# Strassen block products with three token groups in place of plain products for the merge and the MLP of a hybrid recurrent block

## The chip, the cores and the metric

One Trainium2 chip, one of its cores. The metric is the device time of one execution in microseconds. TensorE (PE, with its weight loads PEld), VectorE (DVE), ScalarE (ACT), GpSimd (POOL) and the DMA queues of SyncE (SP) and ScalarE work side by side and wait for each other on semaphores.

## What is computed

One layer over 2048 latent tokens and 256 context tokens of width 1024, then a final norm. The part that matters here is what follows the recurrences:

```python
def branch_merge(h_lru, g, p_mixed, gt, w_lru_out, w_pool_out, w_o):
    lru_out = (h_lru * jax.nn.gelu(g)) @ w_lru_out          # z @ [1024,1024]
    pool_out = p_mixed @ w_pool_out                         # y @ [512,1024]
    g_lru, g_pool = jnp.split(jax.nn.sigmoid(gt), N_BRANCH, axis=-1)
    return (g_lru * lru_out + g_pool * pool_out) @ w_o      # [1024,1024]
...
x = x + gate1[:, None, :] * y_l
x = x + gate2[:, None, :] * sq_relu_mlp(modulate(x, norm2_g[l], shift2, scale2), mlp_w1[l], mlp_w2[l])
...
def sq_relu_mlp(h, w1, w2):                                 # w1 [1024,4096], w2 [4096,1024]
    return jnp.square(jax.nn.relu(h @ w1)) @ w2
```

## The kernel before

Channels stand on the 128 partitions, tokens on the free dimension. Every product of two float32 matrices is run as three float16 passes (high by high, high by low, low by high, `mm3`, L65 to L73) over operands scaled by a power of two (`scale_of`, L75: a POOL all-reduce at L81 and three tiny DVE instructions) and split into halves (`split`, L93: ACT writes the high half at L94, DVE the low half at L95). One matmul takes a 128x128 weight block and 512 tokens.

The first part (to about 1086 us) computes the normed input, the recurrences, the gates and the pool branch. It leaves z (8 tiles of 128 channels), y (4 tiles) and the sigmoid gates s in DRAM. It ends with gate tiles ("fills", L422) whose matmuls read the normed input.

Then comes the second part. y and z are reloaded and split (`reload`, L715); `w_pool_out` with y (L740), `w_lru_out` with z (L758) and the gates give the merged tiles `mt`; `w_o` (L808) adds to x and gives `x1`; `make_h2` norms it. The MLP runs over 16 groups of 256 hidden channels and 4 blocks of 512 tokens: `m1` (L833 takes the result out of PSUM), `m1_split` (DVE and ACT make the two halves of the hidden values), `m2` (L868 adds each product to `x1`). Weights are loaded, scaled and split once (`prep`, L102), a group ahead. POOL has little to do here but all-reduces.

The order on each engine is set by the scheduler of the tile layer from the program's order and its own model of time; SP's DMA queue alone keeps the program's order. Tiles come from pools with a fixed number of buffers, and a new tile waits until an old one's last reader is done.

Of the kernel before, what the change touches and what calls it, by code (L numbers as in the profile page):

```python
# [17 lines left out]
P = 128  # L18
# [21 lines left out]

@with_exitstack
def block_kernel(ctx: ExitStack, tc: tile.TileContext, a):
    """Activations keep channels on partitions and tokens on the free dimension.

    Matrix products run as three float16 passes (hi*hi + hi*lo + lo*hi) over operands that are
    scaled by powers of two taken from their measured magnitude and split into two halves.
    """
# [9 lines left out]
    apool = ctx.enter_context(pool("apool", 1))  # L57
    ring = ctx.enter_context(pool("ring", 4))
# [7 lines left out]
    # ---------------------------------------------------------------- helpers  # L66
# [8 lines left out]
    def scale_of(m, k):  # L75
        with tc.high_priority(offset=PRIO):
            return scale_of_(m, k)

    def scale_of_(m, k):
# [5 lines left out]
        V.tensor_scalar(inv.bitcast(I32), e, 14 << 23, 20 << 23, op0=OP.subtract, op1=OP.max)  # L85
# [16 lines left out]
    def prep(srcs, joint=False, w16=None):  # L102
        """Load chunks [128, n <= 1024]; each gets its own scale, or all of them one."""
# [27 lines left out]
    icnt = cp.tile([P, 5, 64], F32, name="icnt")  # L131
    nc.sync.dma_start(icnt, a["icnt"])
# [19 lines left out]
    # 8*softplus(-lam): max(-lam, 0) + log1p(exp(-|lam|)), log1p(e) = 2 atanh(e / (2 + e))  # L152
# [24 lines left out]
    # ---------------------------------------------------------------- scratch in DRAM  # L177
# [5 lines left out]
    mmax = cp.tile([P, NB, KT], F32, name="mmax")  # L183
# [3 lines left out]
    st = ExitStack()  # L187
    slots = st.enter_context(pool("slots", 10, reuse_waits="tile"))
# [13 lines left out]
    def rstd(total, w, rs):  # L202
        """1 / sqrt(mean + eps) on every partition of sums of squares [128, w] per partition."""
# [6 lines left out]
    def rstd_of(x, w, t_tile):  # L210
        """The same of x [128, 8, w]."""
# [37 lines left out]
    def norm_x(x, w, eng):  # L249
        """Its inverse root mean square and a supply of pieces, both in one slot."""  # L250
# [26 lines left out]
    # shift1 and scale1 for the latent and the context stream  # L277
# [17 lines left out]
    def ada1_pe(wt, cc):  # L295
        """As rows on two partitions, then turned into columns."""
# [11 lines left out]
    def ada1_dve(wt, c):  # L308
        """Products summed over k on VectorE, then over partitions."""
# [30 lines left out]
    def affine(scale, shift, g, m):  # L340
        """Scaled per-channel factor and term of a modulated norm, and the inverse scale."""
# [6 lines left out]
        s, inv = scale_of(bd[:, 0:1], 1)  # L348
# [35 lines left out]
    def ada_piece(q):  # L384
        """gate1, shift2, scale2, gate2 (q = 0..3) of the latent stream."""
# [21 lines left out]
    class Fill:  # L407
        """Sigmoid of one tile of branch-gate channels, kept in DRAM for the merge."""
# [24 lines left out]
    class Lru:  # L433
        """One tile of 128 recurrent channels: conv, gates, both scans, gelu gate."""
# [44 lines left out]
        def gates(self, between=()):  # L479
            """Recurrence and input gates; the products of other tiles go in between."""  # L480
# [59 lines left out]
    # first tiles, token block by token block as the normed input becomes ready  # L540
# [79 lines left out]
    # ---------------------------------------------------------------- pool branch  # L620
# [67 lines left out]
    fetch(("y", 0), a["w_po"][0])  # L688
# [26 lines left out]
    def reload(src, s, hi, lo):  # L715
        for q in range(0, T, 1024):
            raw = ring.tile([P, 1024], F32, name="raw")
            nc.sync.dma_start(raw, src[:, q:q + 1024])
            split(hi[:, q:q + 1024], lo[:, q:q + 1024], raw, s)

    def tokens(b):
        return slice(b * BW, b * BW + BW)

    y16 = ywp.tile([P, 2, 4, T], F16, name="yw")
# [18 lines left out]
    wo16 = ywp.tile([P, KT, 2, 1024], F16, name="yw")
    inv_wo = cp.tile([P, KT], F32, name="inv_wo")
    for n in range(KT):
        if n + 1 < KT:
            fetch(("z", n + 1), a["w_lo"][n + 1])
        (w,), invw = wq.pop(("z", n))
        iv = mul_small(invw, inv_z, 1, "ivf")
        _, iw = prep([a["w_o"][n]], w16=[wo16[:, n]])  # L750
        V.tensor_copy(inv_wo[:, n:n + 1], iw)
        for b in range(NB):
            t = t512()
            nc.sync.dma_start(t, s_d[0][n][:, tokens(b)])
            ps = ptile()
            mm3(ps, wt8(w), [(z16[k // 2][:, 0, k % 2, tokens(b)], z16[k // 2][:, 1, k % 2, tokens(b)])
                             for k in range(KT)])
            V.scalar_tensor_tensor(t, ps, iv, t, op0=OP.mult, op1=OP.mult)  # L758
            V.tensor_tensor(mt[b][:, n, :], mt[b][:, n, :], t, op=OP.add)
            absmax(mmax[:, b, n:n + 1], mt[b][:, n, :])  # L760

    # ================================================================ w_o, residual, second norm
    aff2 = affine(mod2[:, 2, :], mod2[:, 1, :], vc("g2"), 2)
    inv_h2 = aff2[2]
    x1 = []
    h2 = []

    def make_h2(b):
        rs = rstd_of(x1[b], BW, t512)
        t = bpool.tile([P, KT, 2, BW], F16, name=f"B{b}")  # L770
        modulate(x1[b], BW, rs, aff2[0], aff2[1], t, t512)
        h2.append(t)

    NG = 16

    def prep_w1(g):
        w1, inv1 = prep([a["w1"][2 * g], a["w1"][2 * g + 1]], joint=True)
        return w1, mul_small(inv1, inv_h2, 1, "iv1")

    m16s, css = [], []  # L780

    def split_m(b):
        mx = sm.tile([P, 1], F32, name="um")
        absmax(mx, mmax[:, b, :])
        s, inv = scale_of(mx, 1)
        cs = sm.tile([P, KT], F32, name="cs")
        V.scalar_tensor_tensor(cs, inv_wo, inv, mod2[:, 0, :], op0=OP.mult, op1=OP.mult)
        m16 = bpool.tile([P, KT, 2, BW], F16, name=f"B{b}")
        for k in range(KT):
            split(m16[:, k, 0, :], m16[:, k, 1, :], mt[b][:, k, :], s)  # L790
        xt = apool.tile([P, KT, BW], F32, name=f"A{b}")
        nc.sync.dma_start(xt, a["xT"][b])
        x1.append(xt)
        m16s.append(m16)
        css.append(cs)
# [205 lines left out]
```

## Time and profile before

| what | us |
|---|---|
| three runs | 2883.71, 2883.86, 2886.08 |
| median | 2883.86 |
| profiled execution: its span (no other time of it is given) | 2885.5 |
| of it, first part, to the last fill | 1086 |
| of it, second part | 1799 |
| PE busy in the span | 2721.1 |

[...] PE matmuls are pipelined: what one costs in a stream is the distance from one to the next, not its own length.

### The profile page before, as it was taken

How to read it: one execution, taken by the hardware profiler on the slowest of the kernel's cores; microseconds unless marked ns; L12 is line 12 of the kernel's file. 1: busy time of each engine (PE TensorE's matmuls, PEld its weight loads, DVE VectorE, ACT ScalarE, POOL GpSimd, SP SyncE). 2: the span in 40 equal slices, each digit the busy share in tenths (PEclk: the TensorE clock that was granted, in tenths of full speed). 3: DMA queues.
4: the chain of work that ended last, by engine and by line, in shares of the span. 5: the costliest groups of instructions: out<-in, count | busy, mean ns of one | idle time of the engine just before them, and what ended most of it. 6: DMA issues, size and time to landing. Idle time of an engine off the chain costs nothing.

```text
span 2885.5 us, 30620 instructions
## 1 busy us (share of the span) xinstructions
PE 2721.1 (94%) x12496; PEld 1241.8 (43%) x12496; DVE 1904.9 (66%) x2883; ACT 812.7 (28%) x917; POOL 459.1 (16%) x371
## 2 busy tenths in 40 slices
PE   5798988898889999999997999999999999999998
PEld 1344444444334444444443444444444444444444
DVE  4867778875576745676466666666666665656567
ACT  2655564446545232113231111011011110110112
POOL 2713332332322000000331000000000000000022
PEclk7899999999999999999999999999999999999999
DMA  7021123211111136433001000000000000000002
GB/s 304 9 77 59 70 99 113 88 51 55 55 41 40 55 121 222 154 105 132 30 18 56 30 30 29 16 30 25 20 30 30 30 16 29 30 22 23 0 30 88
DMA packets 49165, 177.60 MB, mean 62 GB/s; under 512 B 4736, under 2 KB 7040, under 8 KB 43520
## 3 DMA queue, kind: packets, MB, share of 16 engines
q1 hardware_dynamic: 44992, 146.29, 14.9%
q10 hardware_dynamic: 4032, 29.36, 2.5%
q8 instruction: 97, 1.59, 0.2%
q14 instruction: 44, 0.36, 0.0%
HBM read 137.88 MB, written 37.75 MB: 61 GB/s over the span
## 4 chain that ended last, share of the span: by engine, by line
PE 66%; DVE 13%; issue 7%; ACT 6%; POOL 5%; DMA 3%; SPq 0%; ACTq 0%; DVEq 0%; POOLq 0%
PE mm L72 65%; DVE slot L515 2%; POOL slot L513 2%; POOL sc_g L81 1%; DMA raw<-z 1%; DVE slot L518 1%; DVE slot L512 1%; DVE slot L395 1%; DVE wm L91 1%; POOL slot L535 1%; ACT slot L493 1%; DVE A L868 1%; DVE slot L471 1%; ACT slot L94 1%; POOL slot L257 1%
## 5 line engine op out<-in xcount | busy, mean ns | idle before, releaser
L72 PEld LDWEIGHTS <-w 128*128 128x128 f16 x10944 | 1078.1, 99 | 1387.2 <-issue 136.9
L72 PE MATMUL mm<-B,w 128*128 128x512 f16 x3840 | 845.6, 381 | 15.1 <-ACT B L233 5.3
L72 PE MATMUL mm<-A,w 128*128 128x512 f16 x3408 | 774.3, 388 | 72.2 <-ACT slot L422 56.8
L72 PE MATMUL mm<-h,w 128*128 128x512 f16 (+1 forms) x3120 | 676.4, 376 | 9.7 <-DVE h L858 9.5
L868 DVE SCALAR_TENSOR_TENSOR A<-mm,cs,A 128x512 f32<-128x512 f32 (+1 forms) x520 | 373.6, 738 | 44.2 <-PE mm L72 42.5
L833 DVE TENSOR_SCALAR_CACHE_REDUCE r<-mm 128x512 f32<-128x512 f32 x128 | 88.2, 689 | 309.8 <-PE mm L72 309.7
L855 ACT ACTIVATE h<-r 128x1024 f16<-128x1024 f32 x64 | 67.6, 1056 | 791.4 <-DVE ivs L850 766.0
L94 ACT ACTIVATE w<-raw,sc_s 128x1024 f16<-128x1024 f32 (+1 forms) x116 | 127.1, 1116 | 458.9 <-PE mm L72 260.2
L91 DVE TENSOR_REDUCE wm<-raw 128x1 f32<-128x1024 f32 (+1 forms) x124 | 146.2, 1181 | 123.9 <-DMA raw<-in_w_dram 78.5
L72 PE MATMUL mm<-B,yw 128*128 128x512 f16 x768 | 166.4, 379 | 0.0
L841 POOL PARTITION_ALL_REDUCE hm<-um x64 | 23.1, 361 | 865.9 <-DVE um L839 841.9
L95 DVE SCALAR_TENSOR_TENSOR w<-raw,sc_s,w 128x1024 f16<-128x1024 f32 (+1 forms) x116 | 143.1, 1253 | 26.7 <-ACT w L94 26.2
L72 PE MATMUL mm<-slot,g 128*128 128x512 f16 (+1 forms) x528 | 118.6, 373 | 4.9 <-ACT slot L493 4.9
L81 POOL PARTITION_ALL_REDUCE sc_g<-wm x69 | 65.6, 973 | 308.6 <-DVE wm L91 249.8
L72 PEld LDWEIGHTS <-yw 128*128 128x128 f16 x768 | 75.1, 98 | 91.6 <-issue 1.7
L493 ACT ACTIVATE slot<-mm,vec,ivg 128x512 f32<-128x512 f32 (+1 forms) x160 | 105.0, 743 | 10.9 <-PE mm L72 9.8
L498 POOL TENSOR_TENSOR slot<-slot 128x2312 f32<-128x2312 f32 x16 | 83.6, 5223 | 117.5 <-ACT slot L493 115.3
L94 ACT ACTIVATE slot<-slot,sc_s 128x2312 f16<-128x2312 f32 (+1 forms) x12 | 25.8, 2148 | 258.9 <-DVE sc_s L87 240.2
L512 DVE SCALAR_TENSOR_TENSOR slot<-slot 128x2312 f32<-128x2312 f32 x16 | 41.0, 2562 | 82.7 <-ACT slot L511 82.7
L72 PE MATMUL mm<-yw,w 128*128 128x512 f16 x384 | 83.4, 379 | 0.3 <-DVE w L95 0.2
L72 PEld LDWEIGHTS <-g 128*128 128x128 f16 x528 | 53.9, 102 | 65.5 <-issue 13.1
L858 DVE TENSOR_TENSOR h<-sq,h 128x1024 f16<-128x1024 f32 x64 | 77.9, 1217 | 0.0
(182 smaller groups left out, 2108.1 us busy)
## 6 DMA issues: line engine op xcount, KB each, us to landing
raw<-in_w_dram SPq DMA_DIRECT2D x64, 512.0 KB, 3.2
slot<-in_w_ada_dram SPq DMA_DIRECT2D x22, 1024.0 KB, 5.5
A<-in_xT_dram SPq DMA_DIRECT2D x8, 2048.0 KB, 8.7
t<-s SPq DMA_DIRECT2D x64, 256.0 KB, 3.5
s<-slot ACTq DMA_DIRECT2D x11, 1024.0 KB, 4.0
raw<-in_w_gt_dram SPq DMA_DIRECT2D x16, 512.0 KB, 7.2
z<-slot ACTq DMA_DIRECT2D x8, 1024.0 KB, 5.4
raw<-z SPq DMA_DIRECT2D x16, 512.0 KB, 5.8
```

The source lines that it names most:

```text
L72: TE.matmul(ps, l, r, start=(c == 0), stop=(c == n - 1))
L81: G.partition_all_reduce(g, m, P, ABSMAX)
L91: V.tensor_reduce(out, x, axis=AX.X, op=OP.max, apply_absolute_value=True)
L94: S.activation(hi, x, AF.Copy, scale=s)
L95: V.scalar_tensor_tensor(lo, x, s, hi, op0=OP.mult, op1=OP.subtract)
L493: S.activation(dst[:, o:o + w], ps[:, :w], AF.Sigmoid, bias=vcol("br" if i == 0 else "bi", 8 * d + j), scale=self.ivg)
L498: G.tensor_tensor(I, I, uc, op=OP.mult)
L512: V.scalar_tensor_tensor(Tt, A, 1.0, Tt, op0=OP.add, op1=OP.mult)
L833: V.tensor_scalar(r[:, i, :], ps, 0.0, None, op0=OP.max, op1=OP.max, accum_out=pm[:, i:i + 1])
L855: S.activation(h16[:, 0], r, AF.Square)
L858: V.tensor_tensor(h16[:, 1], sq, h16[:, 0], op=OP.subtract)
L868: V.scalar_tensor_tensor(x1[b][:, n, c], ps, cs[:, n:n + 1], x1[b][:, n, c], op0=OP.mult, op1=OP.add)
```

## The change

The second part is rewritten; the first keeps its instructions. Each weight matrix and each activation is seen as 2x2 blocks, and the product of two such is made of seven block products instead of eight. The sums of blocks that go into the seven are formed ahead: three more weight blocks and three more activation blocks than the four plain ones, each scaled and split. Tokens go in three groups of 684, 684 and 680 (a group's halves are the two column blocks, 342 or 340 wide), and each group goes through merge and MLP. I call the merge of a group M0, M1, M2, and its MLP W0, W1, W2; in the program all merges come first, then all MLPs.

In M0 and W0 each weight unit (1024x128 or alike, `prep_units`) is loaded, its magnitude is taken by ACT, POOL forms the sums (4 instructions of 512 columns), ACT and DVE split seven blocks, and the result (1.8 MB) is stored in DRAM; in M1, M2, W1, W2 it is only loaded (`load_units`). A `Job` is one 2x2 product: its seven products go to three PSUM banks, X (products 1, 6, 4, 7), Y (2) and Z (5, 3), and a bank is read between two products that add to it. `values` takes them out in M's first two products and in m1, `sums` adds them to `x1`. Jobs overlap by four products (`run`).

```diff
-    def scale_of(m, k):
+    def scale_of(m, k, up=14):
...
+    xmp = st.enter_context(pool("xm", 12, reuse_waits="tile"))
+    wup = st.enter_context(pool("wu", 4, reuse_waits="tile"))
+    rawp = st.enter_context(pool("raw7", 2, reuse_waits="tile"))
+    cpl = st.enter_context(pool("C", 8, reuse_waits="tile"))
+    fpl = st.enter_context(pool("F", 2, reuse_waits="tile"))
+    epl = st.enter_context(pool("E", 5, reuse_waits="tile"))
...
+        for k, (r, u) in enumerate(zip(rs, us)):
+            S.activation(u[:, 0, 0:4, :], r[:, 0:4, :], AF.Abs, accum_out=m[:, k:k + 1])
+            sub(G, r[:, 5, :], r[:, 0, :], r[:, 2, :])
+            G.tensor_tensor(r[:, 2, :], r[:, 2, :], r[:, 3, :], op=OP.add)
+            sub(G, r[:, 4, :], r[:, 2, :], r[:, 0, :])
+            sub(G, r[:, 6, :], r[:, 1, :], r[:, 4, :])
...
+            for sl in (slice(0, 4), slice(4, 7)):
+                S.activation(u[:, 0, sl, :], r[:, sl, :], AF.Copy, scale=s)
+                V.scalar_tensor_tensor(u[:, 1, sl, :], r[:, sl, :], s, u[:, 0, sl, :], op0=OP.mult, op1=OP.subtract)
+            if keep:
+                t = dram.tile([P, 2, 7, wd], F16, name=f"st_{kind}{i}")
+                nc.scalar.dma_start(t, u)
...
+    PROD = {1: (0, 0, "X"), 2: (1, 1, "Y"), 3: (6, 2, "Z"), 4: (3, 6, "X"), 5: (2, 3, "Z"), 6: (4, 4, "X"), 7: (5, 5, "X")}
...
+    def run(job):
+        prev = pend[0]
+        for who, n in ((job, 1), (prev, 3), (prev, 7), (job, 5), (job, 2), (prev, 4), (job, 6)):
+            if who is not None:
+                who.product(n)
...
+    def split_f(f, s, w, cuts=((0, 4), (4, 7))):
+        c = c_tile()
+        for lo, hi in cuts:
+            S.activation(c[:, 0, lo:hi, :w], f[:, lo:hi, :], AF.Copy, scale=s)
+            V.scalar_tensor_tensor(c[:, 1, lo:hi, :w], f[:, lo:hi, :], s, c[:, 0, lo:hi, :w],
+                                   op0=OP.mult, op1=OP.subtract)
...
+    def from_dram(srcs, half, g, s):
...
+            t_sums(G, f[:, 0, :], f[:, 1, :], f[:, 2, :], f[:, 3, :], f)
+            out.append(split_f(f, s, w))
...
+    def sums(acc, cs):
+
+        def ev(n, ps):
+            for r, c in {1: [(0, 0)], 2: [(0, 0)], 3: [(0, 1)], 4: [(1, 0)], 5: [(1, 1)], 6: [(0, 1)], 7: [(1, 1)]}[n]:
+                o = acc(r, c)
+                V.scalar_tensor_tensor(o, ps, cs(r), o, op0=OP.mult, op1=OP.add)
...
+                def then(r, c, t, s=s, i=i):
+                    m = self.mt[i + 4 * r][:, c, :]
+                    G.tensor_tensor(t, t, s[r][:, c, :], op=OP.mult)
+                    G.tensor_tensor(m, m, t, op=OP.add)
...
+    for g in range(3):
+        for p in range(8):
+            m1(g, p)
+            if p == 0 and g:
+                m2(g - 1, 7, finisher(g - 1))
...
+            if p:
+                m2(g, p - 1)
+                if p == 7 and g < 2:
+                    make_h2(g + 1)
```

**ACT where the second part begins.** The last fill's sigmoids (`hc`) and the high halves of y (`yw`), before:

```order
L422 ACTIVATE hc_6771<-mm_6772,ivf_6769 128x512
L94 ACTIVATE yw_6888<-raw_6902,ivk4_6899 128x1024
L94 ACTIVATE yw_6888<-raw_6906,ivk4_6899 128x1024
L94 ACTIVATE yw_6888<-raw_6910,ivk4_6899 128x1024
L94 ACTIVATE yw_6888<-raw_6914,ivk4_6899 128x1024
L422 ACTIVATE hc_6771<-mm_6798,ivf_6769 128x512
```

The same place now; C is a split activation tile of seven blocks, F its float32 form:

```order
L431 ACTIVATE hc_6758<-mm_6759,ivf_6756 128x512
L431 ACTIVATE hc_6758<-mm_6785,ivf_6756 128x512
L431 ACTIVATE hc_6758<-mm_6811,ivf_6756 128x512
L431 ACTIVATE hc_6758<-mm_6837,ivf_6756 128x512
L882 ACTIVATE C_6949<-F_6942,ivk4_6917 128x1368
L882 ACTIVATE C_6949<-F_6942,ivk4_6917 128x1026
L882 ACTIVATE C_6961<-F_6954,ivk4_6917 128x1368
```

The splits of y stood between the sigmoids; now all of them stand behind the last.

**POOL in the product with `w_lru_out`.** Before, it has one all-reduce for each weight tile:

```order
L81 ISA sc_g_7048<-wm_7044 128x1
L81 ISA sc_g_7137<-wm_7133 128x1
L81 ISA sc_g_7226<-wm_7222 128x1
L81 ISA sc_g_7315<-wm_7311 128x1
L81 ISA sc_g_7404<-wm_7400 128x1
```

Now, for one weight unit of M0 (raw: the unit's float32 blocks, xm: merged values and gates, E: values out of PSUM):

```order
L717 TENSOR_TENSOR raw_7520<-raw_7520 128x512
L993 TENSOR_TENSOR xm<-xm,E 128x342
L992 TENSOR_TENSOR E<-E,xm 128x342 x3
L90 ISA
L90 ISA sc_g_7529<-wm_7519 128x1
L760 ISA
L760 TENSOR_TENSOR raw_7520<-raw_7520 128x512
L993 TENSOR_TENSOR xm<-xm,E 128x342 x3
L717 TENSOR_TENSOR raw_7520<-raw_7520 128x512
L992 TENSOR_TENSOR E<-E,xm 128x342
L717 TENSOR_TENSOR raw_7520<-raw_7520 128x512
L993 TENSOR_TENSOR xm<-xm,E 128x342
```

The weight sums and the gating of the products share one queue that held neither.

**DVE in the MLP.** Before, in one step of the loop (A is x1):

```order
L868 SCALAR_TENSOR_TENSOR A_9481<-mm,cs_14225,A_9481 128x512
L854 TENSOR_SCALAR r<-r,hq 128x1024
L850 TENSOR_TENSOR ivs<-ivs 128x1
L868 SCALAR_TENSOR_TENSOR A_9481<-mm,cs_14225,A_9481 128x512
L857 TENSOR_TENSOR sq<-r 128x1024
```

Now, in W0, as an m2 ends and an m1 begins (wu: a split weight unit, L944 adds a product to x1):

```order
L944 SCALAR_TENSOR_TENSOR xm_11912<-mm_12684,cs2_12480,xm_11912 128x342
L774 SCALAR_TENSOR_TENSOR wu_12457<-raw7_12454,sc_s1_12469,wu_12457 128x2048
L883 SCALAR_TENSOR_TENSOR C_12563<-F_12299,sc_s1_12559,C_12563 128x1368
L883 SCALAR_TENSOR_TENSOR C_12563<-F_12299,sc_s1_12559,C_12563 128x1026
L944 SCALAR_TENSOR_TENSOR xm_11912<-mm_12684,cs2_12480,xm_11912 128x342
L883 SCALAR_TENSOR_TENSOR C_12568<-F_12418,sc_s1_12559,C_12568 128x1368
```

An addition that frees a PSUM bank now stands behind splits that are up to 2048 elements long.

## Rows read from the trace of the kernel before

**Rows 1.** Page part 1: busy us (share of the span), instructions of each engine.

```profile
PE 2721.1 (94%) x12496; PEld 1241.8 (43%) x12496; DVE 1904.9 (66%) x2883; ACT 812.7 (28%) x917; POOL 459.1 (16%) x371
```

**Rows 2.** Busy time by stage: start:end, length, engines, clock, DMA share, GB/s.

```profile
1086.40:1344.00 257.60, 253.91 (x1163) 113.84 (x1161) 166.67 (x306) 47.05 (x50) 17.03 (x27) 0.99 0.43 137
1344.00:1517.00 173.00, 173.00 (x797) 78.40 (x796) 102.06 (x126) 62.07 (x83) 55.58 (x31) 1.00 0.18 66
1517.00:1600.00 83.00, 61.62 (x261) 26.51 (x260) 54.19 (x106) 17.16 (x21) 9.37 (x12) 0.88 0.13 41
1600.00:2764.00 1164.00, 1164.00 (x5393) 527.70 (x5392) 739.70 (x1473) 125.64 (x116) 37.89 (x86) 1.00 0.07 24
```

**Rows 3.** Chain that ended last, longest piece: start us, length us, what.

```profile
1592.86 1167.39 PE mm L72 x5402
```

**Rows 4.** PE's timeline: last fill, and the last products with 256 columns.

```profile
1065.52 20.88 PE L72 MATMUL mm<-A,w 128*128 128x512 f16 x96
...
2856.44 5.08 PE L72 MATMUL mm<-h,w 128*128 128x256 f16 x45
```

**Rows 5.** DVE groups by shape (busy us, mean ns, idle before), one timeline piece.

```profile
L868 DVE SCALAR_TENSOR_TENSOR A<-mm,cs,A 128x512 f32<-128x512 f32 x504 | 367.2, 747 | 43.2 <-PE mm L72 41.5
L95 DVE SCALAR_TENSOR_TENSOR w<-raw,sc_s,w 128x1024 f16<-128x1024 f32 x108 | 137.2, 1290 | 24.9 <-ACT w L94 24.9
L857 DVE TENSOR_TENSOR sq<-r 128x1024 f32<-128x1024 f32 x64 | 77.8, 1216 | 0.0
L95 DVE SCALAR_TENSOR_TENSOR slot<-slot,sc_s 128x2312 f16<-128x2312 f32 x8 | 21.0, 2627 | 14.1 <-ACT slot L94 14.1
L83 DVE TENSOR_SCALAR sc_e<-sc_g 128x1 int32<-128x1 int32 x122 | 17.5, 148 | 77.1 <-POOL sc_g L81 76.1
...
2860.85 2.35 DVE L868 SCALAR_TENSOR_TENSOR A<-mm,cs,A 128x256 f32<-128x256 f32 x6
```

**Rows 6.** ACT groups by shape: splitting a weight, taking products out of PSUM.

```profile
L94 ACT ACTIVATE w<-raw,sc_s 128x1024 f16<-128x1024 f32 x108 | 121.4, 1145 | 437.8 <-PE mm L72 260.2 <-DVE sc_s L87 74.5 <-DVE ivf L99 61.9
L422 ACT ACTIVATE hc<-mm,ivf 128x512 f32<-128x512 f32 x20 | 13.8, 688 | 48.3 <-PE mm L72 42.2 <-DVE slot L536 6.0
```

**Rows 7.** POOL by line: ns min/median/max, first and last start, forms.

```profile
L257 POOL TENSOR_TENSOR slot<-slot x35: 722/1265/1750, 20.0 to 139.5; 128x512 f32<-128x512 f32 x28, 128x256 f32<-128x256 f32 x7
L81 POOL PARTITION_ALL_REDUCE sc_g<-wmj x32: 355/355/963, 1395.2 to 2634.7; - x32
```

**Rows 8.** Timelines of POOL and DVE at 124 to 132 and 1416 us.

```profile
124.40 8.45 POOL L257 TENSOR_TENSOR slot<-slot 128x512 f32<-128x512 f32 x6
...
124.91 2.88 DVE L240 TENSOR_TENSOR A<-slot,A 128x512 f16<-128x512 f32 x2
127.72 1.75 DVE L315 SCALAR_TENSOR_TENSOR slot<-slot,sil 128x512 f32<-128x512 f32 x1
...
130.52 1.75 DVE L315 SCALAR_TENSOR_TENSOR slot<-slot,sil 128x512 f32<-128x512 f32 x1
...
1416.02 1.72 POOL L237 TENSOR_TENSOR t<-A,t 128x512 f32<-128x512 f32 x1 [0.63 <-DVE B L240]
...
1416.53 0.74 DVE L808 SCALAR_TENSOR_TENSOR A<-mm,cs,A 128x512 f32<-128x512 f32 x1
```

**Rows 9.** DMA: one reload from issue to landing; the busiest stretch.

```profile
raw<-y SPq DMA_DIRECT2D x8, 512.0 KB, 4.4
...
20.00:40.00 20.00, 13.78 (x28) 3.86 (x27) 8.30 (x8) 4.49 (x6) 10.34 (x11) 0.66 1.04 405
```

**Rows 10.** Stretches in which PE waited, as rows 2.

```profile
1540.00:1560.00 20.00, 16.25 (x74) 7.12 (x73) 17.86 (x29) 3.18 (x5) 2.55 (x2) 1.00 0.16 52
...
360.00:380.00 20.00, 12.61 (x47) 5.10 (x46) 16.32 (x17) 9.84 (x11) 5.13 (x2) 0.75 0.42 158
```

**Rows 11.** DVE's timeline behind the last product.

```profile
2870.86 1.74 DVE L904 RECIPROCAL t<-t 128x256 f32<-128x256 f32 x1
2872.63 3.51 DVE L885 SCALAR_TENSOR_TENSOR A<-A,vec,t 128x256 f32<-128x256 f32 x6
```

More of the change, by code (lines that the diff above doesn't have):

```diff
@@ new lines, in load_units @@
+    def load_units(keys):
+        for kind, i in keys:
+            wd = 256 if kind == "po" else HB
+            u = wup.tile([P, 2, 7, HB], F16, name="wu")
+            nc.sync.dma_start(u[:, :, :, :wd], stash[(kind, i)])
+            units[(kind, i)] = u
+    order = []
+    for g in range(3):
+        order += [(g, [(k, i)]) for k in ("po", "lo", "wo") for i in range(4)]
+    for n in range(25):
+        g, q = n // 8, n % 8
+        if n < 24:
+            order += [(g, [("w1", 2 * q)]), (g, [("w1", 2 * q + 1)])]
+        if n:
+            g, q = (n - 1) // 8, (n - 1) % 8
+            order.append((g, [("w2", 2 * q), ("w2", 2 * q + 1)]))
@@ new lines, in block_kernel, with ensure @@
+    place = {(g, k): n for n, (g, ks) in enumerate(order) for k in ks}
+    ahead = [0]
+    def ensure(g, key, more):
+        upto = min(place[(g, key)] + more, len(order) - 1)
+        while ahead[0] <= upto:
+            g_, ks = order[ahead[0]]
+            if g_ == 0:
+                prep_units(ks, True)
+            else:
+                load_units(ks)
+            ahead[0] += 1
+    PROD = {1: (0, 0, "X"), 2: (1, 1, "Y"), 3: (6, 2, "Z"), 4: (3, 6, "X"), 5: (2, 3, "Z"), 6: (4, 4, "X"), 7: (5, 5, "X")}
@@ new lines, in block_kernel, with __init__, product @@
+    class Job:
+        def __init__(self, aop, bop, m, w, ev, done=None):
+            self.aop, self.bop, self.m, self.w = aop, bop, m, w
+            self.ev, self.done, self.ps = ev, done, {}
+        def product(self, n):
+            ao, bo, bank = PROD[n]
+            if bank not in self.ps:
+                self.ps[bank] = ptile()[:, :self.w]
+                first = True
+            else:
+                first = False
+            ps = self.ps[bank]
+            for k in range(self.m):
+                ah, al = self.aop(ao, k)
+                bh, bl = self.bop(bo, k)
+                for i, (l, r) in enumerate(((ah, bh), (ah, bl), (al, bh))):
+                    TE.matmul(ps, l, r, start=(first and k == 0 and i == 0),
+                              stop=(k == self.m - 1 and i == 2),
+                              skip_group_check=(bank != "Y"))
+            self.ev(n, ps)
@@ new lines, in block_kernel, with weights, aop @@
+    pend = [None]
+    def run(job):
[3 more added lines that the diff above has]
+                who.product(n)
+                if n == 4 and who.done:
+                    who.done()
+        pend[0] = job
+    def weights(keys, lo, wd):
+        us = [units[k] for k in keys]
+        def aop(o, k):
+            if len(us) > 1:
+                u, c = us[k], lo
+            else:
+                u, c = us[0], lo + k * 128
+            return u[:, 0, o, c:c + 128], u[:, 1, o, c:c + 128]
+        return aop
@@ L713, in joint_scale @@
         return ks[:, 0:1], ks[:, 1:2]
[L715 to L724, printed above, removed]
+    def from_dram(srcs, half, g, s):
+        w, t0 = GW[g], GT[g]
+        out = []
+        for k in range(half):
+            f = f_tile(w)
+            for src, sl in ((srcs[k], slice(0, 4, 3)), (srcs[k + half], slice(1, 3))):
+                nc.sync.dma_start(f[:, sl, :], src[:, t0:t0 + 2 * w].rearrange("p (c t) -> p c t", c=2))
+            t_sums(G, f[:, 0, :], f[:, 1, :], f[:, 2, :], f[:, 3, :], f)
+            out.append(split_f(f, s, w))
+        return out
@@ L743, in block_kernel @@
[L743 to L760, printed above, removed]
@@ L763, in block_kernel @@
[L763 to L795, printed above, removed]
@@ L927, in block_kernel @@
[L927 to L938 removed]
+    x1_d = [dram.tile([P, KT, 2 * GW[g]], F32, name=f"x1_{g}") for g in range(3)]
+    rs_d = [dram.tile([P, 2, GW[g]], F32, name=f"rs_{g}") for g in range(3)]
@@ new lines, in square_sum, with root @@
+    def square_sum(acc, x, w, first):
+        if first:
+            S.activation(acc, x, AF.Square)
+            return
+        for c in range(2):
+            e = e_tile(w)
+            S.activation(e, x[:, c, :], AF.Square)
+            G.tensor_tensor(acc[:, c, :], acc[:, c, :], e, op=OP.add)
+    def root(acc, w):
+        for c in range(2):
+            ps = psm.tile([P, BW], F32, name="sm")[:, :w]
+            TE.matmul(ps, ones, acc[:, c, :], start=True, stop=True)
+            S.activation(acc[:, c, :], ps, AF.Sqrt, bias=eps, scale=1.0 / D)
+            V.reciprocal(acc[:, c, :], acc[:, c, :])
@@ new lines, in finisher, with after @@
+    def finisher(g):
+        w, t0 = GW[g], GT[g]
+        box = {}
+        def after(nq):
+            if nq == 0:
+                box["acc"] = xm_tile(w)
+            for r in range(2):
+                square_sum(box["acc"], x1[g][nq + 4 * r], w, nq == 0 and r == 0)
+            if nq == 3:
+                root(box["acc"], w)
+                for n in range(KT):
+                    x = x1[g][n]
+                    V.scalar_tensor_tensor(x, x, vcol("fg", n), box["acc"], op0=OP.mult, op1=OP.mult)
+                    nc.scalar.dma_start(a["out"][:, n, t0:t0 + 2 * w].rearrange("p (c t) -> p c t", c=2), x)
+        return after
```

452 lines of the change are left out of this document (289 added, 163 removed).

## The prediction

> **What bounds the kernel now.** I read the page's busy shares first: PE is busy 94% of the span [rows 1]. Then the table by stage, because a mean hides stages: behind 1086.4 us PE is busy all of the time except 21 us between 1517 and 1600 and 3.7 us ahead of 1344, mostly at a clock of 1.00 [rows 2]. The chain that ended last says the same: one piece of 5402 matmuls, 1167.39 us long [rows 3]. So the second part of the kernel is bound by PE, and what it does is 216 ns for each matmul of 512 columns (1167.39/5402). 8064 of them are 1742 us of the 1799 us that this part lasts. DVE is second there: 739.7 of 1164 us in the MLP. POOL has almost nothing to do (37.9 us) [rows 2].
>
> The profiled execution has a span of 2885.5 us. No other time of it is known, and the median of the runs is 1.6 us less, so I take the sum on the span as it stands.
>
> **PE, the term that the change is made for.** Seven products for eight leave 10584 matmuls of 342 (340) columns: 3528 in each group. The trace has none of that width. It has 512 columns, (20.88-0.38)/95 = 0.216 us apart, and 256 columns, (5.08-0.27)/44 = 0.109 us apart (the last matmul's own length taken off) [rows 4]. A straight line between them gives 0.145 us for 342; a weight load of 1241.8 us/12496 = 0.099 us [rows 1] stays under it. 10584 x 0.145 = 1535 us, 207 us less than before. 2 ns more or less in each is 21 us. If nothing else were on the path, the kernel would take 2885.5-207 = 2678 us. All that follows is what comes back.
>
> **Prices.** DVE: an addition out of PSUM is 747 ns at 512 and 392 at 256 columns, so about 0.51 us at 342; a split's low half is 1290 ns for 1024 and 2627 for 2312 elements, so 2.35, 1.82, 1.64 and 1.28 us for 2048, 1536, 1368 and 1026; a sum of two tiles is 1216 ns for 1024, so about 0.52 for 342; a tiny one 0.15 [rows 5]. ACT: 1145 ns for 1024 elements, 688 for 512, so about 1.43, 1.15 and 0.54 us for 1368, 1026 and 342 [rows 6]. POOL: a sum of two tiles is 1265 ns at 512 and 722 at 256, so 0.91 at 342; an all-reduce 355 [rows 7].
>
> **DVE and POOL block each other.** Six POOL sums of 512 take 8.45 us, 1.41 each, and the DVE instructions beside them that read two tiles from SBUF grow from about 0.74 to 1.75 us: they take turns, and a pair costs about 1.7 us, so that of a POOL sum only some 0.25 us lies beside DVE's work. An addition that reads PSUM and one SBUF tile, in the middle of a POOL sum at 1416.53, takes its normal 0.74 [rows 8]. So I count two kinds of DVE work: splits and sums are blocked by POOL (about 1.0 us of each 512-column sum, 0.7 of a 342 one) and block it; additions out of PSUM and tiny instructions aren't. This decides M0 and W0, where POOL forms weight sums.
>
> **The start of M0.** PE's last fill ends at 1086.4 [rows 4]. Before, the next product started at once, since y had been split between the sigmoids; now six tiles of y and z go through two F buffers, and none is split before the last sigmoid, about 1087. First pair: 1.4 us of ACT and 5.8 of DVE to 1094. Then twice: a load of 4.4 us [rows 9], 8 POOL sums of 0.91, the rest of the DVE pieces, about 13 us. Behind them in the queues stands the first weight unit (sum, all-reduce, three tiny instructions, split): about 3 us. PE starts near 1124: **+38 us** (28 to 48).
>
> **The rest of M0.** In the products with `w_pool_out` and `w_lru_out` PE needs 504 x 0.145 = 73 us. POOL needs 13 sums of 256, 48 of 342, 24 of 512 and 9 all-reduces, 9 + 44 + 30 + 3 = 87 us, in one queue with DVE's blocked work (splits 34, sums 8 us). If none of it collides 87 us; if all does 87 + 42, less 0.25 us at some 50 meetings, 117. I take 108, since POOL would always have work waiting: **+35** (14 to 44). With `w_o` PE needs 49 us; POOL 42 (sums for y and z of the next group, squares, two weight units), with about 31 us of blocking work; the third weight unit waits behind them: 68 us, **+19** (0 to 27).
>
> **Between `w_lru_out` and `w_o`** each group must finish its maximum before it can split: addition 0.5, two POOL sums 1.8, two ACT passes 1.7, reduce, all-reduce, tiny ones 1.2, first split 1.1, with semaphores 8 us, and DVE's 13 us of splits that feed the first products: **+12 each, 36** (24 to 54).
>
> **W0.** Its PE work is 371 us. DVE's own: 217 additions into x1 and 48 into F, 135; 88 sums and differences, 52; weight splits of 28 units, 117; splits of hidden tiles, 47; scaling and tiny ones, 43: 394 us. This alone is 23 us over PE. [...] Four units in flight, stored and loaded at 1.8 MB each, are some 11 MB in 57 us, 200 GB/s, under the 405 that a stretch shows [rows 9]; in W1 and W2 it is 7.3 MB in 49 us. I cost the DMAs at nothing; without that cover a unit of 1.8 MB is 4.5 us.
>
> **Changes of group and the MLP's evictions.** The next group's `make_h2` needs buffers that are free only when the old group's last m1 is through: about 50 DVE instructions, 27 us and the waits between them, against some 15 us of matmuls left to PE: **+18** twice and 10 into W0, **46** (10 to 70). In W1 and W2 DVE has 30 us for each pair of hidden tiles, PE 49, but 25 us of it fall into the 24 us of m2, where a bank must be read within two products (1.7 us) and a split ahead of it is 1.64: about 2 us lost for each of 16: **+32** (0 to 60). The tail behind the last product is square, root, two reciprocals and eight scalings of 684 elements, by the pieces that end the trace [rows 11] about **20 us**, 4 more than before.
>
> **Sum.** 1086.4 + 1535 + 38 + 35 + 19 + 36 + 94 + 46 + 32 + 20 = **2941 us**, 2% slower. The gain of 207 us is given back mostly in the first token group, where the weights are prepared.
>
> **Rivals.**
> 1. *The collisions are covered* (faster). POOL's sums fall into DVE's additions out of PSUM (0.41 of its time) and into its waits. Then W0 takes DVE's own 394 (+23), M0 POOL's own 87 (+14) and `w_o` +5: 2941-71-21-14 = 2835. It decides once the three places lose less than 85 us instead of 148. [...] Against: six sums in a row met a DVE instruction each time [rows 8].
> [...]
> 3. *In-order queues compound.* Each engine waits in its queue for another that waits too, so W1 and W2 lose 6 us for each pair, 64 more: 3005. For it: their m2 has DVE full. Against: DVE and PE ran the old MLP without a gap at 0.64 of DVE.
> 4. *The matmuls of 342 columns aren't cheaper.* At 0.16 us, were the load not hidden, PE would take 158 more; 256 columns at 0.109 speak against it [rows 4]. No chance of its own.
>
> **How the numbers follow.** Forecast 0.48, rival 1 0.25, rival 2 0.12, rival 3 0.15. A fifth of rival 1 lies within 0.2% of before or about, since it reaches up to the point named: faster 0.20, same 0.05, slower 0.75 (0.2%, 6 us, is about what a measurement of this kernel can tell from none). All low ends together give 2738, all high ends 3078, but they don't come together; 2830 to 3040 leaves out half of rival 1 and a third of rivals 2 and 3.
>
> **What would show it.** PE's distance between matmuls in W2 near 0.145; PE without work from 1086 to about 1124; POOL busy near its 87 us in 108 in M0; DVE busy over 0.9 in W0, with weight splits of 2048 longer than 2.35 us in the mean, and W0 near 465 us against some 400 for W1 and W2. Weight splits at their own length and W0 under 400 would make me wrong toward rival 1; a clock under 0.9 in W0 toward rival 2; W2 over 440 toward rival 3.

## The result and the profile after

The changed kernel takes 3443.95 us, the middle of three runs (3435.05 to 3449.41), against 2884.97 us: the ratio is 1.193 (1.191 to 1.196). It is slower, as forecast, but by 560 us where the forecast had 57, and far outside its range. (A fourth run took 9283.93 us, far from the others, and is not counted.) The profiled run is that of 3443.95 us, its span is 3441.9 us.

The page's busy shares, which answer to [rows 1]: PE falls from 94% of the span to 77%, and no other engine comes near filling its own.

```profile
PE 2636.1 (77%) x14946; PEld 1505.1 (44%) x14946; DVE 1982.9 (58%) x2755; ACT 1334.8 (39%) x1584; POOL 904.0 (26%) x732
```

Busy time by stage, as [rows 2] (length, busy us and instructions of PE, PEld, DVE, ACT, POOL, granted clock as a share of the full one, DMA share, GB/s). The rows are: the start, the merge of the three token groups (M0, M1, M2), their MLPs (W0, W1, W2), the tail. A stage begins where the count of matmuls that read weight tiles reaches its number, to within 5 us.

```profile
1086.00:1145.00 59.00, 0.00 (x0) 0.00 (x0) 18.00 (x16) 16.62 (x16) 22.98 (x25) 0.54 0.34 107
1145.00:1508.00 363.00, 151.52 (x831) 89.18 (x832) 127.35 (x185) 103.03 (x129) 155.03 (x143) 0.69 0.36 123
1508.00:1688.00 180.00, 128.36 (x845) 83.04 (x844) 79.27 (x119) 57.23 (x94) 81.07 (x87) 0.89 0.58 193
1688.00:1852.00 164.00, 132.18 (x852) 85.25 (x851) 83.25 (x131) 60.67 (x97) 62.22 (x66) 0.91 0.54 193
1852.00:2598.00 746.00, 469.42 (x2689) 282.36 (x2688) 422.03 (x633) 307.35 (x305) 229.86 (x162) 0.79 0.37 137
2598.00:3017.00 419.00, 400.99 (x2693) 263.73 (x2692) 257.45 (x485) 138.40 (x176) 16.74 (x22) 0.98 0.43 162
3017.00:3420.00 403.00, 393.95 (x2703) 262.74 (x2701) 241.63 (x466) 125.97 (x168) 25.80 (x32) 0.99 0.40 151
3420.00:3441.00 21.00, 2.97 (x4) 1.01 (x4) 11.63 (x11) 1.95 (x4) 3.38 (x5) 0.54 0.43 133
```

W1 and W2, where weights are only loaded, are bound by PE and take about what was forecast (822 us for 848). The loss sits in M0 and W0, where the weights are prepared, and there *no* engine is near full: in W0 DVE is busy for 422 of 746 us, PE for 469, POOL for 230. Such a stage is not short of an engine's time but waits along a chain. So the next view is the waits, here of W0 (who waited for whom: us in total, times, longest). The first three rows are POOL's, then DVE, ACT and PE:

```profile
POOL raw L760 <- issue: 142.6, 20, 9.4
POOL sc_g L90 <- issue: 133.7, 22, 7.9
POOL raw L717 <- issue: 63.4, 9, 7.3
...
DVE sc_e L92 <- POOL sc_g L90: 136.3, 24, 15.6
...
ACT wu L773 <- POOL raw L760: 174.0, 14, 15.7
...
PE mm L832 <- ACT wu L773: 116.5, 15, 13.6
```

Read from below: PE waits for the split of a weight unit on ACT, ACT for the unit's sums on POOL, and POOL for "issue", that is for nothing that the profile shows: 340 us in W0. With its 230 busy us POOL is taken for 570 of 746 us, though the page calls it 26% busy. And these 340 us are not idle time beside the path: of the chain that ended last, 39.7% is "issue" in W0 and 44.0% in M0, against 1.0% in W1 and W2. POOL's timeline shows what they are (start, length, instruction, and in brackets the idle time ahead of it):

```profile
2226.96 1.60 POOL L760 TENSOR_TENSOR raw<-raw 128x512 f32<-128x512 f32 x1 [2.13 <-ACT wu L758]
2234.58 0.41 POOL L90 PARTITION_ALL_REDUCE sc_g<-wmj  x1 [6.02 <-issue]
2241.99 4.66 POOL L717 TENSOR_TENSOR raw<-raw 128x512 f32<-128x512 f32 x2 [7.00 <-issue]
2246.85 1.27 POOL L717 TENSOR_TENSOR raw<-raw 128x512 f32<-128x512 f32 x1 [0.21 <-DMA raw<-in_w_dram]
2254.05 0.41 POOL L90 PARTITION_ALL_REDUCE sc_g<-wm  x1 [5.93 <-issue]
2263.72 1.26 POOL L760 TENSOR_TENSOR raw<-raw 128x512 f32<-128x512 f32 x1 [9.26 <-issue]
2265.06 5.89 POOL L717 TENSOR_TENSOR raw<-raw 128x512 f32<-128x512 f32 x3
```

An all-reduce that follows sums starts 6 us late, and the sum that follows an all-reduce 7 to 9 us late. The all-reduce itself is 0.41 us. The trace of before has the same, in its first part, where no term of my sum looked (POOL's timeline again; the last two rows are from the second part, where my terms come from):

```profile
55.42 3.98 POOL L257 TENSOR_TENSOR slot<-slot 128x512 f32<-128x512 f32 x3 [7.62 <-issue]
65.20 0.41 POOL L81 PARTITION_ALL_REDUCE sc_g<-bd  x1 [5.81 <-issue]
65.53 0.76 POOL L81 PARTITION_ALL_REDUCE sc_g<-wm  x2
72.99 2.60 POOL L257 TENSOR_TENSOR slot<-slot 128x512 f32<-128x512 f32 x2 [6.70 <-issue]
...
1395.19 0.41 POOL L81 PARTITION_ALL_REDUCE sc_g<-wmj  x1 [5.80 <-issue]
1575.51 1.26 POOL L237 TENSOR_TENSOR t<-A,t 128x512 f32<-128x512 f32 x1 [7.23 <-issue]
```

An all-reduce right behind an all-reduce starts without idle time (65.53); there and back costs 5.81 + 6.70 = 12.5 us. What stands between the two kinds can be read too. The view of the all-reduce's line lists it, for the kernel before and for the changed one (count, ns min/median/max, first and last start):

```profile
L81 POOLq MODIFY_POOL_CONFIG  x50: 1/6/15, 1.0 to 1562.4; - x50
...
L90 POOLq MODIFY_POOL_CONFIG  x130: 1/7/15, 1.0 to 3055.0; - x130
```

The trace of the changed kernel has two of these between any sum and the all-reduce behind it (53 places), and two more, at the sum's line and of 82 to 83 ns, on the way back (62 places). The other views leave them out, and the time behind them stands as "issue". Between two all-reduces (57 places) there is none. POOL's order in "The change" has an `ISA` without operands at just these places (L90, L760), which its order of before has not. Of the 5.81 us ahead of the all-reduce at 65.20 these two take 15 ns each, of the 6.70 us ahead of the sum at 72.99 83 ns each. What fills the rest no view shows; that it comes with the change from one kind to the other is what the traces show, and what the experiments test.

### The profile page after: what moved, and what is told of

Its sections match the earlier page's. It is cut to its first block, busy times and chain, and to the rows that moved or that the text cites. A ratio compares the mean times of both kernels' runs of the same rounds, so it can differ in the third digit from the quotient of the medians.

```text
span 3441.9 us, 37286 instructions
## 1 busy us (share of the span) xinstructions
PE 2636.1 (77%) x14946; PEld 1505.1 (44%) x14946; DVE 1982.9 (58%) x2755; ACT 1334.8 (39%) x1584; POOL 904.0 (26%) x732
## 4 chain that ended last, share of the span: by engine, by line
PE 38%; issue 21%; DVE 17%; POOL 10%; ACT 9%; DMA 5%; SPq 0%; ACTq 0%; POOLq 0%; DVEq 0%
PE mm L832 29%; PE mm L81 9%; DVE wu L774 2%; POOL raw L717 2%; DMA raw<-in_w_dram 2%; POOL sc_g L90 2%; DVE C L883 2%; DVE slot L524 2%; DVE slot L404 1%; DVE xm L944 1%; ACT wu L773 1%; POOL raw L760 1%; POOL slot L522 1%; POOL F L717 1%; DVE F L717 1%
## 5 line engine op out<-in xcount | busy, mean ns | idle before, releaser
L832 PE MATMUL mm<-C,wu 128*128 128x342 f16 (+1 forms) x10584 | 1670.8, 321 | 657.1 <-ACT wu L773 311.2
L832 PEld LDWEIGHTS <-wu 128*128 128x128 f16 x10584 | 1062.9, 101 | 1266.1 <-ACT wu L773 332.6
L81 PEld LDWEIGHTS <-w 128*128 128x128 f16 x3600 | 358.3, 100 | 496.9 <-issue 104.3
L944 DVE SCALAR_TENSOR_TENSOR xm<-mm,cs,xm 128x342 f32<-128x342 f32 (+1 forms) x672 | 363.2, 567 | 168.4 <-PE mm L832 163.8
L773 ACT ACTIVATE wu<-raw,sc_s 128x2048 f16<-128x2048 f32 (+3 forms) x88 | 149.3, 1716 | 468.7 <-POOL raw L760 320.3
L774 DVE SCALAR_TENSOR_TENSOR wu<-raw,sc_s,wu 128x2048 f16<-128x2048 f32 (+3 forms) x88 | 196.1, 2246 | 206.7 <-ACT wu L773 206.7
L90 POOL PARTITION_ALL_REDUCE sc_g<-um x41 | 17.8, 436 | 1011.1 <-DVE um L1158 737.8
L717 POOL TENSOR_TENSOR raw<-raw 128x512 f32<-128x512 f32 (+1 forms) x132 | 217.3, 1654 | 230.7 <-DMA raw<-in_w_dram 75.1
L717 DVE TENSOR_TENSOR F<-F 128x342 f32<-128x342 f32 (+1 forms) x240 | 130.1, 550 | 62.8 <-ACT F L1145 61.5
L882 ACT ACTIVATE C<-F,sc_s 128x1368 f16<-128x1368 f32 (+1 forms) x96 | 116.0, 1279 | 79.8 <-DVE sc_s L96 79.8
L883 DVE SCALAR_TENSOR_TENSOR C<-F,sc_s,C 128x1368 f16<-128x1368 f32 (+1 forms) x96 | 143.9, 1518 | 0.1
L90 POOL PARTITION_ALL_REDUCE sc_g<-wm x73 | 61.3, 859 | 266.4 <-issue 167.3
L760 POOL TENSOR_TENSOR raw<-raw 128x512 f32<-128x512 f32 (+1 forms) x44 | 58.3, 1326 | 236.0 <-issue 226.7
```

Of the source, the lines that this page charges most:

```text
L81: TE.matmul(ps, l, r, start=(c == 0), stop=(c == n - 1))
L717: e.tensor_tensor(o, x, y, op=OP.subtract)
L760: G.tensor_tensor(r[:, 2, :], r[:, 2, :], r[:, 3, :], op=OP.add)
L773: S.activation(u[:, 0, sl, :], r[:, sl, :], AF.Copy, scale=s)
L774: V.scalar_tensor_tensor(u[:, 1, sl, :], r[:, sl, :], s, u[:, 0, sl, :], op0=OP.mult, op1=OP.subtract)
L832: TE.matmul(ps, l, r, start=(first and k == 0 and i == 0), stop=(k == self.m - 1 and i == 2), skip_group_check=(bank != "Y"))
```

## The experiments

**Theory A**: POOL's changes between sums and all-reduces set the pace of M0 and W0. **Theory B**: the chain of a unit (load, maximum, sums, split) through two raw tiles does, whichever engine works. **Theory C**, the forecast's own: POOL's wide sums block DVE's splits.

**The weight units' all-reduce left out.**

```diff
-        s, inv = scale_of(m, 1, UP)
+        s, inv = scale_of(m, 1, UP, reduce=False)
...
+        else:
+            g = m
```

> Left out: the all-reduce of a weight unit's maximum (36 times, in M0 and W0); each partition is scaled by its own maximum. Sums on POOL, splits, loads and stores stay. Theory A (POOL pays for each change between sums and all-reduce, about 6 us ahead of the all-reduce and 7 us ahead of the next sum, and this queue sets the pace): W0 falls from 740 us to 440 to 490, where DVE's own 416 us bind, M0 from about 415 to about 280, the whole to about 3040 us. Theory C (the forecast's: POOL's wide sums block DVE's splits): those meetings all stay, so W0 stays above 700 us and the whole above 3400.

3074.33 us, 1.066 (1.063 to 1.069) of before: 370 us less than the changed kernel. M0 takes 220 us (363). W0, from the windows:

```profile
1680.00:2232.00 552.00, 438.49 (x2690) 274.33 (x2689) 432.34 (x635) 304.67 (x304) 216.27 (x134) 0.88 0.49 183
```

POOL's sums are all there and still meet DVE's splits (those of 2048 elements take 2567 ns in the mean, 2622 in the changed kernel), so C falls. A stands, but W0 stops at 552 us where A has 440 to 490: something else is late by some 60 to 110 us. Part of it can be A's own, since the eight all-reduces of the hidden tiles are still on POOL in W0.

**The weight sums moved to DVE, the all-reduces left on POOL.**

```diff
-            sub(G, r[:, 5, :], r[:, 0, :], r[:, 2, :])
+            sub(V, r[:, 5, :], r[:, 0, :], r[:, 2, :])
...
-            sub(G, r[:, 6, :], r[:, 1, :], r[:, 4, :])
+            sub(V, r[:, 6, :], r[:, 1, :], r[:, 4, :])
```

> The four sums of a weight unit go from POOL to DVE; the all-reduces stay on POOL. In W0 POOL then has almost only all-reduces and no change of kind; in M0 it still alternates between the merge's products and all-reduces. DVE gets 112 sums of 512 in W0, about 0.6 us each, 67 us. Theory A: W0 480 to 540 us, M0 nearly as long as it was, the whole about 3200. Theory B (the unit's chain load, maximum, sums, split through two buffers sets the pace, whichever engine does them): the sums shorten the chain by about 5 us of some 45, W0 650 to 700, the whole about 3380.

3168.79 us, 1.099 (1.095 to 1.102). In W0 every all-reduce is kept, but with nothing between them it costs what it lasts. W0, then three rows of POOL's timeline in it:

```profile
1783.00:2320.00 537.00, 430.45 (x2689) 268.82 (x2688) 452.41 (x754) 304.21 (x304) 28.68 (x36) 0.91 0.50 188
```

```profile
2017.69 0.35 POOL L90 PARTITION_ALL_REDUCE sc_g<-wm  x1 [8.10 <-DVE xm L944]
2017.95 0.43 POOL L90 PARTITION_ALL_REDUCE sc_g<-um  x1
2050.11 0.71 POOL L90 PARTITION_ALL_REDUCE sc_g<-wmj  x1 [31.74 <-DVE wmj L765]
```

Now POOL waits almost only for others (7 us of "issue" in W0), and W0 is where A has it (480 to 540), far from B's 650 to 700. M0, where POOL still alternates with the merge's products, keeps 299 of its 363 us. So it is the change of kind that costs, not the all-reduce. The run also gives the size of the collisions: DVE's groups in W0, without POOL's sums and, below, in the changed kernel with them (count | busy us, mean ns):

```profile
L774 DVE SCALAR_TENSOR_TENSOR wu<-raw,sc_s,wu 128x2048 f16<-128x2048 f32 x31 | 73.5, 2371 | 9.4 <-ACT wu L773 9.3
L774 DVE SCALAR_TENSOR_TENSOR wu<-raw,sc_s,wu 128x1536 f16<-128x1536 f32 x31 | 57.4, 1853 | 0.0
L717 DVE TENSOR_TENSOR F<-F 128x342 f32<-128x342 f32 x88 | 44.2, 511 | 0.7 <-ACT F L1145 0.2
...
L883 DVE SCALAR_TENSOR_TENSOR C<-F,sc_s,C 128x1368 f16<-128x1368 f32 x16 | 26.2, 1640 | 0.0
```

```profile
L774 DVE SCALAR_TENSOR_TENSOR wu<-raw,sc_s,wu 128x2048 f16<-128x2048 f32 x31 | 81.3, 2622 | 97.3 <-ACT wu L773 97.3
L774 DVE SCALAR_TENSOR_TENSOR wu<-raw,sc_s,wu 128x1536 f16<-128x1536 f32 x31 | 63.1, 2036 | 22.0 <-ACT wu L773 22.0
L717 DVE TENSOR_TENSOR F<-F 128x342 f32<-128x342 f32 x88 | 53.9, 623 | 7.0 <-ACT F L1145 6.4
L883 DVE SCALAR_TENSOR_TENSOR C<-F,sc_s,C 128x1368 f16<-128x1368 f32 x16 | 30.7, 1920 | 0.0
```

The differences are 7.8 + 5.7 + 9.7 + 4.5 = 28 us. Additions out of PSUM (L944) take 565 ns beside POOL's sums and 571 without: as forecast, they are not held up.

**A dose: every second unit of w1 without its all-reduce.**

```diff
+        if keys[0][0] == "w1" and keys[0][1] % 2:
+            s, inv = last_w1[0]
+        else:
             s, inv = scale_of(m, 1, UP)
```

> A dose: every second unit of w1 takes the scale of the unit ahead of it, so 8 of the 24 weight all-reduces of W0 go, all else stays. Theory A: 8 changes there and back of 13 to 14 us less, W0 630 us, the whole about 3335. Theory B: 8 of 32 units have a shorter chain, two of which overlap: about 50 us less. Theory C: no change.

3361.63 us, 1.165 (1.160 to 1.171); W0 takes 673 us. At the all-reduce's line the changed kernel has 130 of the `MODIFY_POOL_CONFIG`, this one 114, the first experiment 68, two for each change: so 8 changes there and back are gone here and 31 there. They save 82 and 370 us of the whole, 10 and 12 us each. The effect is in proportion, and each change is worth nearly the 12.5 us that POOL loses by it. Between A and B the dose alone does not decide: the 73 us that W0 lost lie between A's 110 and B's 50. The moved sums decide it.

**A fixed scale for weight units, without maximum and all-reduce.**

```diff
-            S.activation(u[:, 0, 0:4, :], r[:, 0:4, :], AF.Abs, accum_out=m[:, k:k + 1])
-        s, inv = scale_of(m, 1, UP)
+        s, inv = w_s, w_inv
...
+    V.memset(w_s, 2.0 ** 7)
+    V.memset(w_inv, 2.0 ** -7)
```

> A fixed power of two as the scale of all weight units: no maximum on ACT, no all-reduce, no tiny instructions. Theory A: as without the all-reduce alone, since ACT is not the bound: about 3030 us, W0 430 to 480. If theory B holds beside A, the shorter chain (2 us of ACT and the waits around it) gives 40 us or more beyond the kernel without the all-reduce alone.

3039.75 us, 1.054 (1.050 to 1.058), 35 us less than with the maximum; W0 is 513 us (552), with DVE busy for 425 (432). The shorter chain helps by a little less than the 40 us that B asked for. So B is not shown beside A; 35 us is what the maximum, the tiny instructions behind it and their waits are worth together.

**All reductions of the second part on PE.** A product with a matrix of ones sums over the partitions; POOL does sums only.

```diff
-        G.partition_all_reduce(g, m, P, ABSMAX)
+        g = psm.tile([P, BW], F32, name="sm")[:, :1]
+        TE.matmul(g, ones, m, start=True, stop=True)
```

> The reductions of the second part (weight units, merged tiles, hidden tiles) go from POOL's all-reduce to a product with a matrix of ones on PE, one column, and a sum takes the place of the maximum; POOL keeps its sums and never changes kind. Theory A (POOL's changes): M0 and W0 as without the weight all-reduces or a little less, since the 11 reductions of merged and hidden tiles change kind no longer: about 3040 to 3060 us. Rival: the product stands in PE's queue and waits there for ACT's maximum, with the matmuls behind it; at 5 us for each of 47 that is 235 us, and the whole stays near 3250.

3016.71 us, 1.045 (1.042 to 1.048), better than A's figure of 3040 to 3060 and far from the rival's 3250. W0:

```profile
1669.00:2173.00 504.00, 427.94 (x2754) 275.43 (x2752) 423.76 (x634) 306.88 (x306) 192.37 (x126) 0.92 0.54 200
```

It is 48 us below the first experiment, which had left the eight all-reduces of the hidden tiles on POOL. How much of the 48 is theirs is not shown: the fixed scale left them there too and came to 513. Of W0's chain 6.0% is now "issue" (39.7% in the changed kernel). The rival's wait in PE's queue is small: it shows in M0 (six waits for a weight unit's maximum, 34.5 us in total, and one of 12.7 for the merged tiles'), and in W0 it comes to 7 us.

**In addition sums on DVE, except those of w1, and z loaded later.**

```diff
+            e = G if keys[0][0] == "w1" else V
...
+                if self.g == 0 and i == 1:
+                    self.load_z()
```

> As the kernel with the reductions on PE, and in addition: the sums of weight units go to DVE except those of w1, and z is loaded and split behind the second unit of w_pool_out instead of ahead of the first. With POOL's changes gone, POOL is busy nearly all of M0's first 100 us, and PE waits there for sums. If POOL's own work is what is late next in M0: start 59 to about 35 us, M0 220 to 180, W0 (half of the sums on DVE, fewer meetings) 550 to 530, the whole about 2970. If DVE is late next: no gain, 3050.

3048.93 us, 1.057 (1.053 to 1.060). The start falls from 44 to 14 us, further than the 35 expected. M0 becomes 231 us instead of 216 and W0 547 instead of 504, and the whole meets the figure for "DVE is late next" (3050). Sums given to DVE cost more (43 us of W0) than their collisions on POOL (the 28 us above). The run moves two things at once; that the later z is not what costs is seen below, where z is moved without the sums and M0 is 211 us, W0 502.

**Without the loads of w1 and w2**, from the kernel with all weight sums on DVE.

```diff
+            fresh = len(raws) < 2 or kind not in ("w1", "w2")
+            if fresh:
+                raws.append(rawp.tile([P, 7, HB], F32, name="raw7"))
+            else:
+                raws.append(raws[-2])
...
+            if fresh:
+                for sl, src in unit_sources(kind, i):
```

> From the kernel with all weight sums on DVE. Left out: the loads of w1 and w2 in W0; the two raw tiles keep what they hold. DVE, ACT, POOL and PE do the same work. It asks what holds W0 at 537 us when POOL is out of it. If DVE's occupation does (452 of 537 us busy): W0 stays above 515. If the chain of a unit through two raw tiles does (load of 8 to 10 us, then maximum, sums, split): W0 falls to 450 to 490.

3131.34 us, 1.085 (1.082 to 1.089). W0 is 502 us instead of 537, between the two cases: the loads held it up by 35 us. In the remaining 502 DVE is busy for 449; that it sets them is not shown.

**The loads of y and z moved.** In the changed kernel PE waits 31.3 us in one piece in M1. PE's waits there, then SP's queue in that time:

```profile
PE mm L832 <- DMA wu<-st_wo: 31.3, 1, 31.3
```

```profile
1627.42 25.34 SPq L902 DMA_DIRECT2D F<-z  x8
1652.81 0.94 SPq L784 DMA_DIRECT2D wu<-st_wo  x2
1653.85 11.45 SPq L784 DMA_DIRECT2D wu<-st_po  x2
```

The weight unit's load stands behind loads of the next group's z, which wait for F buffers.

```diff
                 ensure(self.g, ("po", i), 2)
+                if i == 1:
+                    self.load_z()
...
                 ensure(self.g, ("wo", i), 2)
+                if i == 1 and nxt:
+                    nxt.load_y()
...
-            stages[g + 1].load_y()
-            stages[g + 1].load_z()
```

> From the kernel with the reductions on PE. Moved only: a group's loads of z go behind its second unit of w_pool_out, and the next group's loads of y behind the second unit of w_o; before, both stood on SP's queue, waiting for F buffers, ahead of weight loads. In the trace PE waits 31 us for the load of a w_o unit in the second group and starts M0 only 45 us after the first part. Theory (these loads hold weight loads back): start 45 to about 15, M1 177 to about 145, M2 some 10 less, the whole 2935 to 2950. Rival: z is then late for w_lru_out, and the time comes back there: 3000 or more.

2972.14 us, 1.030 (1.027 to 1.032). The start is 19 us (44), M1 151 (176), but M2 159 (147): what M1 gained is half given back there, and the whole misses the 2935 to 2950 that were expected.

**With that, work shifted between DVE and POOL.**

```diff
+            e = V if keys[0][0] == "lo" and k_odd(keys) else G
...
-            t_sums(V, f[:, 0, :], f[:, 1, :], f[:, 2, :], f[:, 3, :], f)
+            t_sums(G if g == 0 else V, f[:, 0, :], f[:, 1, :], f[:, 2, :], f[:, 3, :], f)
```

> As the kernel with the reductions on PE and the loads moved, and two shifts of work: every second weight unit of w_lru_out has its sums on DVE, and in the first MLP group the 64 sums of hidden tiles go from DVE to POOL (0.51 us each on DVE, 0.9 on POOL). If W0 is bound by DVE's occupation: 33 us of work less, 15 to 30 us off W0. If meetings of POOL and DVE give it back: within 10 us of the kernel without these shifts.

2957.69 us, 1.025 (1.022 to 1.028), the best of all these and still behind the kernel before. W0 is 496 us (502) with DVE's work down from 425 to 403: 22 us of DVE bought 6 of the stage and not 15 to 30, so DVE's occupation alone doesn't set it. What binds those last 100 us over PE's 390 stays open; no single wait is large.

**The moved loads alone**, on the changed kernel, with the edit shown above for them.

> The moved loads alone on the changed kernel, with all POOL all-reduces as they are. Theory: the start and M1 gain as they do with the reductions on PE, 30 us each, but in M0 POOL's changes set the pace, so that an earlier start is given back there: 3444 to about 3400 us. If the loads were the main loss and POOL's changes only fill the wait: below 3300.

The same moves alone give 3404.74 us, 1.180 (1.176 to 1.183): M1 takes 158 us instead of 180 and the start 29 instead of 59, M0 keeps its 363 with POOL's changes in it. The theory's figure was met.

## Why the prediction was right and wrong

Its terms by stage, in us: as forecast (2688 or 840 matmuls of 0.145 and the terms of the sum), in the changed kernel, with the reductions on PE, and with loads and sums moved too.

| | forecast | after | reductions on PE | and moved |
|---|---|---|---|---|
| start | 38 | 59 | 44 | 14 |
| M0 (122+35+19+12) | 188 | 363 | 216 | 211 |
| M1 and M2 (2 x 134) | 268 | 344 | 323 | 310 |
| W0 (390+94+10) | 494 | 746 | 504 | 496 |
| W1 and W2 (780+32+36) | 848 | 822 | 822 | 818 |
| tail | 20 | 22 | 21 | 22 |

With 1086 us ahead of them the columns give 2942, 3442, 3016 and 2957.

**The step that failed** is the price of POOL: "an all-reduce 355" ns [rows 7]. Most of those rows come from the MLP, in which POOL does almost nothing but all-reduces, while the change puts sums between them, and I asked of the two kinds only how long each lasts, not what lies between one and the other. The price was in reach: the first of those very rows (1395.19) stands behind a sum and starts 5.80 us late, four changes there and back lie in the stretch of the second part in which PE waited longest, 1517 to 1600 us [rows 2], and the view that [rows 7] is taken from lists `MODIFY_POOL_CONFIG` beside them. With 12.5 us for there and back, read from the trace of before, M0's nine all-reduces of `w_pool_out` and `w_lru_out` would have added some 110 us to the 87 us that I gave POOL, and W0's 32 some 400 to about 153 (112 sums of 1.265 us and 32 all-reduces of 0.355): past the 465 that the forecast has for W0 (371 + 94), so POOL would have been named the bound. The 87 and the 153 us count busy time, and the time of a change is not busy time. This one step is worth about 430 us of the error of 500 (3442 less 3016), which is what moving the reductions takes out; most of the rest lies in M1 and M2.

**Collisions** were forecast as the main loss of W0: 71 of the 94 us that the sum has for it, the other 23 being DVE's own 394 over PE's 371. No run shows the 71. Collisions exist at the places named, but measure 28 us, and they were not on the path while POOL's queue was; what W0 lost in their place, 242 us (746 less 504), went with POOL's changes. Rival 1, which is their absence, would have been further off still (2835 us). That W0 comes out near the forecast once POOL no longer changes kind (504 and 494) is partly luck. Its collisions are nearer 28 us than 71, and lie elsewhere than I had put them: weight splits are back at 2381 and 1855 ns, and the sums of hidden tiles grow to 704. Against that stand waits for weight loads that I had costed at nothing (35 us where the sums are on DVE), and DVE, which was to fill the stage, is busy for 424 of the 504 us.

**Rival 2** named the clock, under 0.9 in W0. It fell to 0.79 there and 0.69 in M0, and PE's work of W0 grew to 469 us against 401 in W1. But with the reductions on PE it is 0.92 and 0.83, with the same matmuls: the fall follows the waits, it didn't make them.

**Rival 3** had the right mechanism, queues in order that wait for each other, at the wrong place. W1 and W2 took 822 us of the 848 that even the forecast gave them; the chain ran through POOL in M0 and W0, and through SP's queue in M1, where one load stood behind eight others.

**What held**: the matmul of 342 columns. The chain that ended last has two long pieces in W1 and W2,

```profile
2676.09 278.88 PE mm L832 x1920
...
3096.72 321.35 PE mm L832 x2226
```

that is 278.88/1920 = 0.145 and 321.35/2226 = 0.144 us. W1 and W2, the tail and DVE's splits without POOL beside it (2371 and 1853 ns for 2.35 and 1.82 us) came as priced. An addition out of PSUM took 0.57 us instead of 0.51. M1 and M2 take 55 us more than forecast even with the reductions on PE. Moving the loads of y and z takes some 13 of them off, which is SP's queue; the rest stays open.

The direction held, and as forecast it is mostly the first token group that gives the gain of 207 us back, but for another reason than the one forecast: 426 us of the loss were POOL's changes. Even the best kernel here gives back 280.

## What to carry to other kernels

When work is moved onto an engine that runs another kind of instruction, look in the whole trace for that pair side by side and read the idle time between the two, not only their lengths. Where an engine looks idle and its waits say "issue", look whether the chain that ended last runs through that idle time; if it does, it is a price. Where no engine of a stage is near full, follow who waits for whom to the end before pricing any engine's load. And ask of each load that is queued early what is queued behind it.

## What the hardware showed that I had not expected

POOL pays for each change between sums and an all-reduce, every time: in the whole trace of the changed kernel no all-reduce behind a sum starts less than 5.7 us after it (53 of them), and no sum behind an all-reduce less than 6.6 us (62). Where POOL waited for nothing else, that is 38 waits of 234.9 us in total ahead of all-reduces between 1086 and 2620 us of the changed kernel, 6.2 us each, and 42 of 296.9 us ahead of sums of weights, 7.1 us each. A fill of a constant right behind an all-reduce does not pay: at all six such places of each trace, before and changed, it starts without idle time, and there is no `MODIFY_POOL_CONFIG` between the two (POOL's timeline of before):

```profile
944.27 0.76 POOL L81 PARTITION_ALL_REDUCE sc_g<-wm  x2
944.89 0.38 POOL L630 MEMSET slot<- 128x256 f32 x1
```

PE made a reduction over 128 partitions (a sum in place of the maximum) with one matmul of one column, two records of 0.59 us together at 1433 us of the kernel with the reductions on PE, and in W0 its queue waited only 7 us in total for these.
